# Who makes the first chunk's block sums, and in which order w2's operands come, in a Hymba-style layer on one core

## The chip, the cores and the metric

The kernel runs on one core of a Trainium2 chip. The metric is the device time of one launch in microseconds (us); smaller is better. The engines are named as the profile names them: PE (TensorE's matmuls), PEld (its weight loads), DVE (VectorE), ACT (ScalarE), POOL (GpSimd) and SP (the queue that issues most DMAs).

## The reference, cut to what matters

One layer of a decoder trunk for 1024 tokens of width 1024 in float32. It has two SwiGLU feed-forward networks (width 2816) around a mixer of attention and a gated recurrence:

```python
x = x + 0.5 * _swiglu(_rms_norm(x, ffn1_norm), ffn1_w1, ffn1_w3, ffn1_w2)
...                                   # mixer: attention and HGRN2, one output projection
x = x + 0.5 * _swiglu(_rms_norm(x, ffn2_norm), ffn2_w1, ffn2_w3, ffn2_w2)

def _swiglu(h, w1, w3, w2):
    return (jax.nn.silu(h @ w1) * (h @ w3)) @ w2
```

The change touches the last product of a SwiGLU, the one with w2, at its start. As there are two networks, it acts at two places of the run.

## The kernel before

**Precision and products.** Every float32 operand is split into a high part (a CAST on ACT, line 108) and a low part (a subtraction, line 109, on DVE or POOL), and each product of two operands is three matmuls: high by high, high by low, low by high. A block product is a Strassen-like scheme with seven products in place of eight, numbered 0 to 6. The operands of a product are sums and differences of blocks.

**hidden()** makes silu(h w1) * (h w3) in eleven steps `fp`, each with two halves `wi`; its outputs are turned into the seven operands `g` of the next product by tail() (POOL sums on lines 312 to 317, splits on ACT and DVE) and stored to DRAM tensors `gd`.

**back()** is the product with w2, for both networks. The inner dimension is cut into four chunks (`CHUNKS = (3, 3, 3, 2)`), the tokens into four groups q. A round r is one chunk; group(r, q, cs) multiplies the products `cs` of one token group: for each product c the stored operand `gp` comes back by DMA (fetch, line 600, eight products ahead) and is the stationary side, and w2's operand `o{c}` is the moving side; each such product is nine matmuls of 128x512 (line 637; six in the last chunk). Banks: products 0 and 1 accumulate in bank `ya`, 4, 5, 6 in `yb`, 3 and 2 in `yc`. After product 0, ACT copies bank `ya` to a total (line 617) *before* product 1 may accumulate in it; the other banks are copied or added to `acc` on ACT (622) and DVE (624).

**w2's operands.** load() brings four blocks of a chunk, here called by their places (0,0), (0,1), (1,0), (1,1). step(ch, c) splits the source block of product c into `o{c}`. Three of the sources are sums made in place. prep() makes the first ones per piece k: (0,1) = (1,1) - (0,1) on line 553, then (0,0) = (0,1) + (0,0) on line 554; they are what products 5 and 4 read. others() makes the later ones: (1,0) = (1,0) - (0,0) on line 563 and (0,0) = (1,1) - (0,0) on line 564, for products 6 and 3. So others() must come after product 4's and product 1's splits have read the blocks.

**Order.** Inside `manual_schedule` each engine runs its instructions in the order in which they are recorded. At the start of back() the code loads chunk 0 of w2, fetches the first eight `gp`, records the splits of products 0, 2 and 1 and prep(0), and mixes in what is left of hidden(): `before[0]`, `before[1]` (the last two evacuations, lines 362 and 365 on DVE and 278 on POOL) and `before[2]` (the last tail()), whose pieces go into a list `todo`. work() takes pieces from `todo`, done() all that a product needs. The tail's first piece is the split into a tile named `spare`, whose source is the POOL sum of line 312.

**Which products come first.** TURN sets from which group on a product belongs to a round: in round 0 the groups hold products 0 and 2; 0, 4, 1 and 2; 0, 4, 1, 5, 3 and 2; and all seven.

Of the kernel before, what the change touches and what calls it, by code (L numbers as in the profile page):

```python
# [56 lines left out]
CHUNKS = (3, 3, 3, 2)  # L57
# [28 lines left out]
def hymba_kernel(ctx: ExitStack, tc: tile.TileContext, a, out, stop=None):  # L86
    nc = tc.nc
# [434 lines left out]
    def back(i, load, spots, sg, wa, wb, wc, go, so, ac, ps, before, fetch_x, add_x, moments, finish, final):  # L522
# [12 lines left out]
        def sooner(n):  # L535
            for _ in range(n):
                if early:
                    early.pop(0)()
# [4 lines left out]
            while any(w[0] == (ch, c) for w in todo):  # L543
                work(1)

        def prep(ch):

            b11, b12, b22 = b[ch][0, 0], b[ch][0, 1], b[ch][1, 1]

            def first(k):  # L550
                def go():
                    done(ch, 0)
                    nc.gpsimd.tensor_sub(b12[k], b22[k], b12[k])  # L553
                    nc.gpsimd.tensor_add(b11[k], b12[k], b11[k])
                return go

            early.extend(first(k) for k in range(CHUNKS[ch]))
# [9 lines left out]
        def step(ch, c, eng=None):  # L567

            b11, b12, b21, b22 = (b[ch].get(e) for e in ((0, 0), (0, 1), (1, 0), (1, 1)))
            src = {0: b11, 4: b11, 1: b21, 5: b12, 3: b11, 6: b21, 2: b22}[c]  # L570
            o = ops[ch, c] = so.tile([P, 3, 2, 512], F32R, tag=f"o{c}", name=f"o{c}_{ch}")

            def piece(k):
                def go():
                    if c == 4:
                        sooner(len(early))
                    split(o[:, k, 0, :], o[:, k, 1, :], src[k], eng)
                    if c == 1 and ch:
                        others(ch, k)()
                return go  # L580

            todo.extend(((ch, c), piece(k)) for k in range(CHUNKS[ch]))
# [2 lines left out]
        seq = []  # L585
        for r in range(nch + 1):
            for q in range(4):
                cs = [(c, r if q >= TURN[c] else r - 1) for c in ORDER]
                seq.append((r, q, [(c, ch) for c, ch in cs if 0 <= ch < nch]))
        flat_seq = [(q, c, ch) for r, q, cs in seq for c, ch in cs]  # L590
        parts = {}
# [81 lines left out]
                add_x(acc[m // 2][:, m % 2 * 512:m % 2 * 512 + 512], xt.pop(m))  # L673

        with tc.manual_schedule(engines=ORDEREDY):
            b[0] = load(0, ((0, 0), (1, 1), (0, 1), (1, 0)))
            for k in range(AHEAD):
                fetch(k)
            step(0, 0, nc.gpsimd)
            step(0, 2)  # L680
            step(0, 1)
            work(len(todo))
            prep(0)
            sooner(len(early))
            before[0]()
            before[1]()
            rest = before[2]()
            step(0, 4)

            spare = so.tile([P, 3, 2, 512], F32R, tag="o6", name="spare")  # L690
            spots.extend([lambda k=k: [flat(spare[:, k])] for k in range(2)] +
                         [lambda t=t: [acc[t].bitcast(F32R)] for t in (2 * TOKENS[3], 2 * TOKENS[3] + 1)] +
                         3 * [lambda: [wb.tile([P, 512], F32R, tag="c", name=f"go_{m}", bufs=NC) for m in range(2)]])
            todo.extend((None, f) for f in rest[:3])
            todo.extend(((0, 3), others(0, k)) for k in range(CHUNKS[0]))
            todo.extend((None, f) for f in rest[3:])
            for c in (5, 3, 6):
                step(0, c)
            for r, q, cs in seq:
                group(r, q, cs)  # L700
                moments.get((r - nch, q), lambda: None)()
                if (r, q) == (nch - 1, 3) or r == nch and q < 3:
                    todo.extend((None, f) for f in finish(2 * TOKENS[q] + 1, 2 * TOKENS[q], acc))
            final(work)
# [792 lines left out]
```

## Time and profile before

| what | value |
|---|---|
| median of 3 runs | 2055.58 us (2055.48 to 2057.73) |
| the profiled execution's own time | 2058.68 us |
| its span, first to last instruction | 2056.8 us |
| PE busy | 1966.5 us, 96% of the span, 9344 matmuls |
| DVE busy | 1328.2 us, 65% |
| ACT busy | 751.0 us, 37% |
| POOL busy | 827.2 us, 40% |
| mean granted TensorE clock | 0.984 of full speed |

The times of the trace are us from the first instruction. The first network's product with w2 begins at 483.7 us, the second one's at 1822.4 us. A share of busy time is an average over stages; what the change can move is read at those two places.

### The profile page before, as it was taken

How to read it: one execution, taken by the hardware profiler on the slowest of the kernel's cores; microseconds unless marked ns; L12 is line 12 of the kernel's file. 1: busy time of each engine (PE TensorE's matmuls, PEld its weight loads, DVE VectorE, ACT ScalarE, POOL GpSimd, SP SyncE). 2: the span in 40 equal slices, each digit the busy share in tenths (PEclk: the TensorE clock that was granted, in tenths of full speed). 3: DMA queues.
4: the chain of work that ended last, by engine and by line, in shares of the span. 5: the costliest groups of instructions: out<-in, count | busy, mean ns of one | idle time of the engine just before them, and what ended most of it. 6: DMA issues, size and time to landing. Idle time of an engine off the chain costs nothing. (4 is left out here: it accounts for less than half of the span.)

```text
span 2056.8 us, 25751 instructions
## 1 busy us (share of the span) xinstructions
PE 1966.5 (96%) x9344; PEld 1620.4 (79%) x9344; DVE 1328.2 (65%) x2044; ACT 751.0 (37%) x1373; POOL 827.2 (40%) x698
## 2 busy tenths in 40 slices
PE   6889999998999989999999998989899999989998
PEld 5678888886788778888899997777688888867886
DVE  8566766678566665565666767364667666775664
ACT  6333334334311243323434435143343343353112
POOL 6555655556333340000222222053555555664452
PEclk9999999999999999999999999999999999999999
DMA  3144444447887521111001002321444444478875
GB/s 143 41 154 154 143 144 155 153 149 266 295 289 236 198 98 39 35 39 47 16 17 31 9 1 94 132 83 41 145 159 148 144 145 158 143 268 301 290 233 191
DMA packets 160878, 284.07 MB, mean 138 GB/s; under 512 B 10865, under 2 KB 90225, under 8 KB 160753
## 3 DMA queue, kind: packets, MB, share of 16 engines
q1 hardware_dynamic: 158160, 273.53, 39.8%
q10 hardware_dynamic: 2592, 8.91, 1.1%
q8 instruction: 74, 1.21, 0.2%
q14 instruction: 52, 0.42, 0.1%
HBM read 189.08 MB, written 93.32 MB: 137 GB/s over the span
## 5 line engine op out<-in xcount | busy, mean ns | idle before, releaser
L255 PE MATMUL bb<-cb,wparts 128*128 128x512 f32 x1584 | 398.8, 401 | 24.3 <-DVE u L350 12.9
L255 PEld LDWEIGHTS bb<-cb,wparts 128*128 128x128 f32 x1584 | 301.5, 191 | 101.6 <-ACT wparts L108 13.6
L255 PE MATMUL ba<-cb,wparts 128*128 128x512 f32 x1056 | 263.5, 400 | 5.3 <-DVE cb L170 2.6
L255 PE MATMUL bc<-cb,wparts 128*128 128x512 f32 x1056 | 261.6, 396 | 0.0
L255 PEld LDWEIGHTS ba<-cb,wparts 128*128 128x128 f32 x1056 | 200.9, 191 | 54.9 <-DVE cb L170 2.9
L255 PEld LDWEIGHTS bc<-cb,wparts 128*128 128x128 f32 x1056 | 199.0, 189 | 48.9 <-DVE wparts L109 0.4
L109 DVE TENSOR_TENSOR wparts<-s,wparts 128x512 fp32r<-128x512 f32 x176 | 153.4, 874 | 98.6 <-ACT wparts L108 98.6
L637 PE MATMUL yb<-o,gp 128*128 128x512 f32 x792 | 203.9, 400 | 8.9 <-DVE o L109 7.9
L637 PEld LDWEIGHTS yb<-o,gp 128*128 128x128 f32 x792 | 149.2, 189 | 48.2 <-DVE o L109 11.2
L972 PE MATMUL pj<-hH,hw 128*128 128x512 f32 x480 | 171.0, 413 | 4.8 <-ACT hw L108 3.6
L108 ACT CAST o<-b 128x512 fp32r<-128x512 f32 x148 | 83.6, 621 | 246.6 <-PE yb L637 172.1
L109 DVE TENSOR_TENSOR go<-g,go 128x512 fp32r<-128x512 f32 (+1 forms) x152 | 155.5, 1028 | 14.5 <-ACT go L108 14.4
L109 DVE TENSOR_TENSOR wparts<-raw,wparts 128x512 fp32r<-128x512 f32 x116 | 117.3, 1012 | 43.9 <-ACT wparts L108 42.7
L109 DVE TENSOR_TENSOR o<-b,o 128x512 fp32r<-128x512 f32 x144 | 129.4, 911 | 17.4 <-ACT o L108 17.3
L637 PE MATMUL yc<-o,gp 128*128 128x512 f32 x528 | 135.5, 398 | 3.6 <-DVE acc L624 1.6
L1147 PE MATMUL apj<-aw,hH 128*128 128x384 f32 x512 | 138.8, 352 | 0.0
L637 PE MATMUL ya<-o,gp 128*128 128x512 f32 x528 | 135.7, 400 | 2.9 <-ACT ya L617 2.9
L108 ACT CAST wparts<-s 128x512 fp32r<-128x512 f32 x176 | 106.0, 618 | 78.6 <-POOL s L338 37.8
L338 POOL TENSOR_TENSOR s<-raw 128x512 f32<-128x512 f32 x44 | 70.7, 1608 | 147.3 <-DVE wparts L109 87.8
L637 PEld LDWEIGHTS yc<-o,gp 128*128 128x128 f32 x528 | 99.6, 189 | 29.9 <-ACT o L108 2.5
L637 PEld LDWEIGHTS ya<-o,gp 128*128 128x128 f32 x528 | 100.2, 190 | 28.2 <-ACT ya L617 3.3
L972 PEld LDWEIGHTS pj<-hH,hw 128*128 128x128 f32 x480 | 91.7, 191 | 24.9 <-ACT hw L108 3.8
(256 smaller groups left out, 3358.2 us busy)
## 6 DMA issues: line engine op xcount, KB each, us to landing
gd<-go SPq DMA_DIRECT2D x140, 512.0 KB, 3.2
gp<-gd SPq DMA_DIRECT2D x168, 384.0 KB, 4.8
raw<-in_ffn_w SPq DMA_DIRECT2D x88, 512.0 KB, 3.7
b<-in_ffn_w SPq DMA_DIRECT2D x22, 768.0 KB, 7.0
gp<-gd SPq DMA_DIRECT2D x56, 256.0 KB, 3.0
hraw<-in_w_hg SPq DMA_DIRECT2D x32, 256.0 KB, 2.6
araw<-in_w_at SPq DMA_DIRECT2D x16, 384.0 KB, 3.1
b<-in_ffn_w SPq DMA_DIRECT2D x10, 512.0 KB, 5.3
```

The source lines that it names most:

```text
L108: nc.scalar.copy(rhi, src)
L109: (eng or nc.vector).tensor_sub(rlo, src, rhi.bitcast(F32))
L255: mm(bank, w[:, wj, ks], cb[c][:, :, bj, ks], start=(start and k == 0 and (wj, bj) == (0, 0)), stop=(k == 3 and wj == 1), skip_group_check ...
L338: nc.gpsimd.tensor_tensor(out=s[j], in0=s[0] if x is None else x, in1=s[1] if y is None else y, op=getattr(ALU, op))
L637: mm(bank[x], v[:, k, wj, :], o[:, k, bj, :], start=(new and k == 0 and (wj, bj) == (0, 0)), stop=(k == n - 1 and wj == 1), skip_group_che ...
L972: mm(u[hf], w[k // 4][:, wj, k % 4, :], r[hf][:, k, :], start=(k == 0 and (wj, r) == (0, hH)), stop=(k == KT - 1 and wj == 1))
L1147: mm(pj, l[t // 4][:, k, tsl], w[:, j, :], start=(n == 0), stop=(n == 3 * KT - 1))
```

## The change

In the first chunk of w2, in both networks: prep(0) records its six sums (lines 553, 554) on DVE where they were on POOL; others(0, k) are recorded at once where they were spread in `todo` after three pieces of the tail; the block (0,1) is loaded second and (1,1) third; product 4's split comes before product 1's; products 5, 3 and 6 are split in the order 5, 3, 6 as before, but with one piece of the tail after 5 and the other pieces after 3; and in the first two groups of round 0 the products run in the order 0, 2, 4, 1 (before: 0, 4, 1, 2). All other chunks stay as they were.

```diff
-        def prep(ch):
+        def prep(ch, eng=nc.gpsimd):
...
-                    nc.gpsimd.tensor_sub(b12[k], b22[k], b12[k])
-                    nc.gpsimd.tensor_add(b11[k], b12[k], b11[k])
+                    eng.tensor_sub(b12[k], b22[k], b12[k])
+                    eng.tensor_add(b11[k], b12[k], b11[k])
...
-                cs = [(c, r if q >= TURN[c] else r - 1) for c in ORDER]
+
+                cs = [(c, r if q >= TURN[c] else r - 1) for c in (ORDER if r or q > 1 else (0, 2, 4, 1))]
...
-            b[0] = load(0, ((0, 0), (1, 1), (0, 1), (1, 0)))
+            b[0] = load(0, ((0, 0), (0, 1), (1, 1), (1, 0)))
             for k in range(AHEAD):
                 fetch(k)
             step(0, 0, nc.gpsimd)
             step(0, 2)
+            work(len(todo))
+            prep(0, nc.vector)
+            sooner(len(early))
+            step(0, 4)
             step(0, 1)
             work(len(todo))
-            prep(0)
-            sooner(len(early))
+            for k in range(CHUNKS[0]):
+                others(0, k)()
             before[0]()
             before[1]()
             rest = before[2]()
-            step(0, 4)
...
-            todo.extend((None, f) for f in rest[:3])
-            todo.extend(((0, 3), others(0, k)) for k in range(CHUNKS[0]))
-            todo.extend((None, f) for f in rest[3:])
-            for c in (5, 3, 6):
-                step(0, c)
+            step(0, 5)
+            todo.append((None, rest[0]))
+            step(0, 3)
+            todo.extend((None, f) for f in rest[1:])
+            step(0, 6)
```

What this does to three engines' orders at the start of back() in the first network (the second is alike). `b00`, `b01`, `b10`, `b11` are the tiles that hold the blocks, `g10_..` the last step's gates, `o4_0` product 4's operand of chunk 0.

POOL before, from the last piece of product 0's low part on:

```order
L109 TENSOR_TENSOR o0_0_3774<-b00_0__3749,o0_0_3774 128x512
L553 TENSOR_TENSOR b01_0_3754<-b11_0_3752,b01_0_3754 128x512
L554 TENSOR_TENSOR b00_0_3748<-b01_0_3754,b00_0_3748 128x512
...
L278 TENSOR_TENSOR g10_1_3555<-g10_1_3555,c110_1_3620 128x512
L278 TENSOR_TENSOR g10_0_3509<-g10_0_3509,u210_1_3642 128x512
L312 TENSOR_TENSOR g10_0_3509<-g10_0_3509,g10_1_3555 128x512
...
L563 TENSOR_TENSOR b10_0_3756<-b10_0_3756,b00_0_3748 128x512
```

and with the change:

```order
L109 TENSOR_TENSOR o0_0_3774<-b00_0__3749,o0_0_3774 128x512
L563 TENSOR_TENSOR b10_0_3756<-b10_0_3756,b00_0_3748 128x512
L564 TENSOR_TENSOR b00_0_3748<-b11_0_3754,b00_0_3748 128x512
...
L278 TENSOR_TENSOR g10_1_3555<-g10_1_3555,c110_1_3620 128x512
L278 TENSOR_TENSOR g10_0_3509<-g10_0_3509,u210_1_3642 128x512
L312 TENSOR_TENSOR g10_0_3509<-g10_0_3509,g10_1_3555 128x512
```

Six instructions stood ahead of the gates' last products (278) and the sum of line 312, and six stand there now; but these are the later sums, which wait for product 4's and product 1's splits, and the first sums are gone to DVE.

DVE with the change, from product 2's low part on (before, product 1's low part came next, then lines 362 and 365, then product 4's):

```order
L109 TENSOR_TENSOR o2_0_3775<-b11_0_3754,o2_0_3775 128x512 x3
L553 TENSOR_TENSOR b01_0_3752<-b11_0_3754,b01_0_3752 128x512
L554 TENSOR_TENSOR b00_0_3748<-b01_0_3752,b00_0_3748 128x512
...
L109 TENSOR_TENSOR o4_0_3794<-b00_0_3748,o4_0_3794 128x512 x2
L109 TENSOR_TENSOR o4_0_3794<-b00_0__3749,o4_0_3794 128x512
L109 TENSOR_TENSOR o1_0_3795<-b10_0_3756,o1_0_3795 128x512 x3
L362 TENSOR_TENSOR c110_1_3620<-bb10_1_3625,c110_1_3620 128x512
L365 TENSOR_TENSOR u210_1_3642<-bc10_1_3680,u210_1_3642 128x512
L109 TENSOR_TENSOR o5_0_3822<-b01_0_3752,o5_0_3822 128x512 x3
```

The six sums now stand between product 2's and product 4's low parts, and product 5's low part comes ahead of the tail's.

ACT with the change, from the copy of the first `ya` bank on:

```order
L618 COPY ya0_3837<-ya0_0_3827 128x512
...
L108 CAST spare_3821<-g10_0_3509 128x4x128
L618 COPY ya1_3873<-ya0_1_3863 128x512
L108 CAST o3_0_3823<-b00_0_3748 128x512 x2
...
L623 COPY acc0_7_3738<-yb0_1_3900 128x512 x2
...
L618 COPY ya2_3958<-ya0_2_3948 128x512
```

The cast into `spare` stands directly ahead of the second `ya` copy, as it did before; ahead of the third `ya` copy stand now also product 3's casts, the second piece of the tail and the two copies of `acc0_7`, which wait for a DVE addition.

On SP the load of (0,1) moves up past five stores of `gd` (from behind them to ahead of them), the other two loads keep their places, the `gp` of product 2 for the second group moves ahead of those of 4 and 1, and two later `gp` move ahead of stores from `spare`.

## Rows read from the trace of the kernel before

**Rows 1.** Windows: both w2 starts, and 1 us of TensorE's slow stretch; PEclk is granted clock.
```profile
483.70:520.90 37.20, 30.04 (x110) 21.80 (x109) 30.84 (x29) 17.36 (x35) 23.96 (x16) 0.91 0.82 278
1822.40:1858.20 35.80, 28.61 (x110) 20.95 (x109) 27.13 (x28) 17.41 (x36) 24.91 (x17) 0.95 0.83 282
...
63.00:64.00 1.00, 1.00 (x4) 0.81 (x3) 0.83 (x2) 0.47 (x1) 0.00 (x0) 0.50 0.00 0
```

**Rows 2.** Timeline of PE, first network: start, length, what, [idle before <-releaser].
```profile
483.71 2.26 PE L637 MATMUL ya<-o,gp 128*128 128x512 f32 x9
...
492.51 0.95 PE L637 MATMUL yb<-o,gp 128*128 128x512 f32 x3 [2.10 <-DVE o L109]
...
496.90 2.66 PE L637 MATMUL ya<-o,gp 128*128 128x512 f32 x9
...
510.78 3.27 PE L637 MATMUL yb<-o,gp 128*128 128x512 f32 x8 [2.59 <-DVE o L109]
...
518.67 2.37 PE L637 MATMUL yc<-o,gp 128*128 128x512 f32 x9 [0.78 <-DVE acc L624]
520.88 2.26 PE L637 MATMUL ya<-o,gp 128*128 128x512 f32 x9
```

**Rows 3.** Timeline of PE, second network.
```profile
1822.37 2.26 PE L637 MATMUL ya<-o,gp 128*128 128x512 f32 x9
...
1835.24 3.75 PE L637 MATMUL ya<-o,gp 128*128 128x512 f32 x9 [2.87 <-ACT ya L617]
...
1858.16 2.26 PE L637 MATMUL ya<-o,gp 128*128 128x512 f32 x9
```

**Rows 4.** Timeline of DVE, first network.
```profile
479.04 0.69 DVE L278 TENSOR_TENSOR g<-g,u 128x512 f32<-128x512 f32 x1
479.65 10.31 DVE L109 TENSOR_TENSOR o<-b,o 128x512 fp32r<-128x512 f32 x6
489.89 0.68 DVE L362 TENSOR_TENSOR c<-bb,c 128x512 f32<-128x512 f32 x1
490.49 0.68 DVE L365 TENSOR_TENSOR u<-bc,u 128x512 f32<-128x512 f32 x1
...
510.05 2.49 DVE L109 TENSOR_TENSOR o<-b,o 128x512 fp32r<-128x512 f32 x4
```

**Rows 5.** Timeline of POOL, first network.
```profile
479.27 1.61 POOL L553 TENSOR_TENSOR b<-b,b 128x512 f32<-128x512 f32 x1 [1.05 <-DMA b<-in_ffn_w]
...
487.79 1.63 POOL L554 TENSOR_TENSOR b__3749<-b,b__3749 128x512 f32<-128x512 f32 x1
...
493.67 1.60 POOL L312 TENSOR_TENSOR g<-g,g 128x512 f32<-128x512 f32 x1
...
531.59 1.30 POOL L553 TENSOR_TENSOR b<-b,b 128x512 f32<-128x512 f32 x1 [22.08 <-DMA gp<-gd]
...
534.22 1.29 POOL L553 TENSOR_TENSOR b<-b,b 128x512 f32<-128x512 f32 x1
```

**Rows 6.** Timeline of ACT, first network.
```profile
477.13 1.67 ACT L108 CAST o<-b 128x512 fp32r<-128x512 f32 x3 [2.24 <-DMA b<-in_ffn_w]
...
486.01 0.59 ACT L617 COPY ya<-ya 128x512 f32<-128x512 f32 x1 [3.15 <-PE ya L637]
486.49 0.59 ACT L622 COPY acc<-ya 128x512 f32<-128x512 f32 x1
...
495.31 0.62 ACT L108 CAST spare<-g 128x512 fp32r<-128x512 f32 x1 [5.24 <-POOL g L312]
495.83 0.58 ACT L617 COPY ya<-ya 128x512 f32<-128x512 f32 x1
...
501.64 1.35 ACT L108 CAST go<-g 128x256 fp32r<-128x256 f32 x4
```

**Rows 7.** Timeline of PE after its longest idle stretch, early in the run.
```profile
61.95 5.49 PE L255 MATMUL bb<-cb,wparts 128*128 128x512 f32 x12 [8.64 <-ACT wparts L108]
...
70.25 2.96 PE L255 MATMUL bb<-cb,wparts 128*128 128x512 f32 x12
```

## The prediction

> **What bounds the kernel now.** TensorE sets the end of this run; it stands still in few places, and two of them are the starts of the product with w2. I read first the windows over these two stretches: PE is busy 30.04 of 37.20 us in the first network and 28.61 of 35.80 in the second [rows 1]. Then the timeline of PE, which says what a gap costs in all. Nine matmuls of one product are due every 2.10 us (each row of nine is 2.26 long with the tail of its last matmul, and the next row starts 2.10 later where nothing waits). Twelve products lie between the first w2 matmul and the first one of the fourth token group, so that one should come 12 x 2.10 = 25.2 us after the first. It comes at 520.88 - 483.71 = 37.17 us in the first network [rows 2] and at 1858.16 - 1822.37 = 35.79 us in the second [rows 3]. So 12.0 and 10.6 us are lost, **22.6 us in all, the most that any change here can win**. From there on PE is the engine that the others wait for, so I take it that what is won or lost up to this point moves the end one for one.
>
> The reader should see three waits in it. Product 4's operand is late: PE idles 2.10 us for DVE's low parts [rows 2], because POOL's six first sums run from 479.27 to 489.42 [rows 5]. Then the second `ya` product of the group starts at 496.90 and 1835.24; in the second network the view names its releaser, ACT's copy of line 617 [rows 3]. That copy stands in ACT's queue right behind the cast into `spare`, and this cast waited until 495.31 for the POOL sum of line 312 [rows 6], which ended at 493.67 + 1.60 = 495.27 [rows 5]. So a piece of the old network's tail, for which nobody is in a hurry, holds a copy for which PE waits. Third, product 5's and 3's operands are late: 2.59 us idle and eight matmuls at 3.27 us [rows 2].
>
> **Prices.** DVE's subtraction of two SBUF tiles takes 2.49 / 4 = 0.62 us while POOL idles and 10.31 / 6 = 1.72 us while it works [rows 4]. POOL's takes (534.22 - 531.59) / 2 = 1.31 us while DVE idles, and (487.79 - 479.27) / 5 = 1.70 us beside DVE [rows 5]. DVE's readings of PSUM stay at 490.49 - 489.89 = 0.60 us beside POOL [rows 4]. An ACT copy takes 486.49 - 486.01 = 0.48 us, a cast 495.83 - 495.31 = 0.52 [rows 6].
>
> **The change part by part**, with the first network's times; z is the first w2 matmul, 483.71.
>
> (1) First sums on DVE. DVE is free for product 2's low parts at 479.65, as now [rows 4]; its casts began at 477.13 [rows 6]. POOL has ended product 0's low parts 1.05 us before 479.27 [rows 5] and now has nothing to do, so DVE runs at its fast price: three low parts, 1.9, to 481.5; six sums, three of them waiting for the one before (I take the full length of 0.69 for these [rows 4]), 3.9, to 485.5; product 4's three low parts to 487.3. Product 4 is first wanted at z + 4 x 2.10 = 492.1, since product 2 now goes ahead of it. **The wait for product 4 is gone**, with 4.8 us to spare. The first low part of product 1 is done at 487.95.
>
> (2) Later sums on POOL. They overwrite what product 1's low parts read, so POOL starts at 488.0 and not before. Beside it DVE has two low parts of product 1, the two PSUM readings of lines 362 and 365, and three low parts of product 5: 2 x 1.72 + 2 x 0.60 + 3 x 1.72 = 9.8, to 497.75. In the 8.6 us of SBUF work POOL does 8.6 / 1.70 = 5.0 sums and in the 1.2 us beside PSUM work 0.9, so its sixth ends at about 497.8. Behind it, alone: two products of line 278 and the sum of line 312, 3 x 1.31 = 3.95, to 501.75. Before, this sum ended at 495.27: **the tail's first sum is 6.5 us later**.
>
> (3) What waits behind it. In ACT's queue the cast into `spare` still stands ahead of the second `ya` copy, and PE needs that copy for product 1. From the sum's end to PE it took 0.04 + 0.52 + 0.58 [rows 5, 6], and with 0.06 for the semaphore 1.2, so PE goes on at 502.95, z + 19.2. It ran dry at z + 5 x 2.10 = 494.2: an idle stretch of 8.7 us. The nearest row is the early one of 8.64: after it 24 matmuls took 70.25 - 61.95 = 8.30 us where 24 x 0.233 = 5.60 was due [rows 7], 2.7 us more, at a granted clock of 0.50 [rows 1], TensorE's lower level of 1.2 GHz. So the third group starts at z + 19.2 + 2.1 + 2.7 = z + 24.0, and its second product ends at z + 28.2.
>
> (4) The third `ya` copy. Ahead of it ACT has copies that wait for DVE's addition to `acc0_6`, and that stands behind one low part of the tail, three of product 3 and another of the tail. From 502.4 on: two and a half of these beside POOL's last three sums, the rest alone, and the addition, 1.72 + 1.72 + 1.2 + 2 x 0.62 + 0.6, to 508.9. Then ACT's three copies, two casts, four short casts at 1.35 in all [rows 6] and the copy itself at 0.58, 4.4, to 513.3 = z + 29.6. PE waits 1.4 us for it. After the gap of 2.10 us three matmuls took 0.95 [rows 2], about full pace, so I count no clock here.
>
> (5) To the fourth group: three products, 6.3; the wait of the next one for DVE's addition, 0.78 before [rows 2], taken as 0.8 to 0.9; and one product, 2.1: **z + 38.8**. Products 5 and 3 no longer wait: their low parts are done at 497.75 and about 507.7.
>
> (6) The rest costs nothing. The load of (0,1) goes ahead of five stores, and POOL, which waited for it at 479.27 [rows 5], no longer does; SP's other moves follow the order in which PE now reads the operands. Twelve more operations on DVE, fewer on POOL, are inside (1). The late tail feeds stores that only the last chunk reads back.
>
> **The sum.** z + 38.8 against 37.17 and 35.79: 1.6 and 3.0 us later, 4.6 in all. The second network comes out the same after the change, since POOL's idle time removes what made the two differ. The sum is a difference inside the profiled execution (2058.68 us, span 2056.8); that lies 3.1 above the median of the runs shown, and I add it to the median: 2055.58 + 4.6 = **2060.2 us**. Of 22.6 us lost the change takes away about 10, at products 4, 5 and 3, and puts some 14 back at the `ya` copies. A difference within 0.2% (4.1 us) is about what a measurement of this kernel cannot tell from none, and the forecast is just beyond it.
>
> **Bounds.** The step that decides is POOL's pace from 488.0 to the sum of line 312. If all nine operations took 1.31, PE would go on 1.9 us sooner, and with 0.8 from (4) a start would be 2.7 shorter. If all nine took 1.70, it would be 1.2 longer. The nearest rows are the mixed ones, so I take 1.70 beside DVE. The clock after 8.7 us idle lies between 1.2 us (the eight matmuls of 510.78, 3.27 for 2.03) and 2.7; but up to 1.4 of that only shortens the wait in (4).
>
> The Trainium skill (SBUF — State Buffer, section Who interferes with whom) says that a DVE instruction with two SBUF inputs and a GpSimd one that reads SBUF take turns, the second one blocked until the first has finished. By that a pair would take 0.62 + 1.31 = 1.93 us, and the eight pairs of (2) to (4) 0.2 us more each, 1.6 per start and 2063.4 in all. The trace agrees that both slow down, but with 1.72 and 1.70 us for a pair; the rows decide.
>
> **Rivals.**
> - *The tail's sum is not late* (chance 0.07). If ACT's second `ya` copy were free of the `spare` cast, or the sum came ahead of the later sums, only the wait of 0.9 would be left at each start: 11.1 + 9.7 = 20.8 won, 2034.8 us. For it speaks only that (1) works; against it that the order shows the cast ahead of the copy and six sums ahead of line 312, and that ACT has already waited 5.24 us in this very place [rows 6]. It decides at z + 10.5: were the copy done by then, all would be won; each us later costs one.
> - *POOL is fast* (0.16). With nine operations at 1.31 a start ends at z + 36.1, 1.1 sooner than before in the first network and 0.3 later in the second: 2054.8, no change. The point from which it decides is the sum's end at 499.3. Against it: DVE has five SBUF operations in just that stretch.
> - *The second gap drops the clock too* (0.12). If the wait of (4) is 2.6 us or more, eight matmuls cost 1.24 more, as at 510.78 [rows 2]; twice, 2062.7.
> - *Full blocking* (0.05), 2063.4, as above.
>
> **How the numbers follow.** The forecast has 0.60; its own spread is about 2.5 us to either side, so 0.33 of it lies beyond 2059.7. With the two slower rivals, slower by over 0.2% has 0.50. The rest of the forecast, 0.27, and most of the fast POOL, 0.13, are within 0.2%: 0.40. Faster: 0.07 and 0.03, 0.10. The range leaves out the first rival and the ends of the others: 2055.2 to 2064.0.
>
> **What would show it.** Right: in both w2 starts one gap of 8 to 9 us ahead of the second group's product 1, released by ACT's `ya` copy, and a second of 1 to 2 us ahead of the third group's; no wait for product 4; DVE's six sums at 0.6 to 0.7 us; POOL's line 563 beginning 4 us after z and line 312 ending 18 us after it; the fourth group at z + 38 to 40. Wrong: the fourth group well below z + 36, or a `ya` copy that does not wait for POOL; or a wait for `gp`.

## The result and the profile after

The changed kernel takes **2068.55 us** (median of 4 runs, 2067.70 to 2069.75); beside it the kernel before took 2055.53 us (4 runs, 2054.20 to 2057.73). The ratio is 1.006, with a 95% interval of 1.0048 to 1.0072: slower by 0.6%, some 13 us. The forecast was 2060.2 us, with a range up to 2064.0. So the sign was right and the size was not. The profiled execution took 2069.75 us, its span is 2068.0 us, 11.2 more than the span of the kernel before.

The head of the page: the span, and busy time of each engine with its share and instructions.

```profile
span 2068.0 us, 25755 instructions
...
PE 1968.7 (95%) x9344; PEld 1625.7 (79%) x9344; DVE 1317.6 (64%) x2056; ACT 750.8 (36%) x1373; POOL 806.9 (39%) x686
```

The timeline of PE over the first start of w2 (start and length in us, what, and in brackets the idle time before it and its releaser), the counterpart of [rows 2]; z, the first w2 matmul, is 482.83 here:

```profile
482.83 2.26 PE L638 MATMUL ya<-o,gp 128*128 128x512 f32 x9
...
491.23 2.26 PE L638 MATMUL yb<-o,gp 128*128 128x512 f32 x9
502.16 5.85 PE L638 MATMUL ya<-o,gp 128*128 128x512 f32 x18 [8.67 <-ACT ya L618]
507.85 2.26 PE L638 MATMUL yb<-o,gp 128*128 128x512 f32 x9
512.44 3.73 PE L638 MATMUL ya<-o,gp 128*128 128x512 f32 x9 [2.33 <-ACT ya L618]
516.01 2.26 PE L638 MATMUL yb<-o,gp 128*128 128x512 f32 x9
...
521.22 2.37 PE L638 MATMUL yc<-o,gp 128*128 128x512 f32 x9 [0.85 <-DVE acc L625]
523.42 2.26 PE L638 MATMUL ya<-o,gp 128*128 128x512 f32 x9
```

Product 4 (`yb`, 491.23) no longer waits. Two gaps are left, both released by ACT's `ya` copy: 8.67 us ahead of the second group's product 1 and 2.33 us ahead of the third group's. Behind each of them TensorE is slow: 18 matmuls take 507.85 - 502.16 = 5.69 us where 4.20 are due, and nine take 516.01 - 512.44 = 3.57 where 2.10 are due. The fourth group comes at z + 40.59, 3.4 us later than in [rows 2].

The second network, counterpart of [rows 3], does the same, and the fourth group comes at 1868.08 - 1827.33 = z + 40.75, 5.0 us later than before:

```profile
1827.33 2.26 PE L638 MATMUL ya<-o,gp 128*128 128x512 f32 x9
...
1846.66 6.01 PE L638 MATMUL ya<-o,gp 128*128 128x512 f32 x18 [8.67 <-ACT ya L618]
...
1856.93 3.89 PE L638 MATMUL ya<-o,gp 128*128 128x512 f32 x9 [2.16 <-ACT ya L618]
...
1868.08 2.26 PE L638 MATMUL ya<-o,gp 128*128 128x512 f32 x9
```

The granted clock over the stretches behind the two gaps of the first network (columns: stretch, us, busy us of PE, PEld, DVE, ACT and POOL with instructions, PEclk, DMA share, GB/s):

```profile
502.16:507.85 5.69, 5.69 (x18) 4.54 (x19) 5.69 (x6) 2.51 (x5) 3.46 (x3) 0.73 0.52 164
...
512.44:516.01 3.57, 3.57 (x10) 2.85 (x10) 2.07 (x5) 2.08 (x5) 0.00 (x0) 0.58 1.02 298
```

Where the first gap comes from, in the timelines of DVE, POOL and ACT, the counterparts of [rows 4 to 6]. DVE's last first sum, product 5's low parts, and later the addition to `acc`:

```profile
484.14 0.69 DVE L554 TENSOR_TENSOR b__3749<-b,b__3749 128x512 f32<-128x512 f32 x1
...
490.67 4.06 DVE L109 TENSOR_TENSOR o<-b,o 128x512 fp32r<-128x512 f32 x3
...
507.38 0.68 DVE L625 TENSOR_TENSOR acc<-yb,acc 128x512 f32<-128x512 f32 x1
```

POOL's first and last later sum, and the sum of line 312 behind them:

```profile
487.37 1.63 POOL L563 TENSOR_TENSOR b<-b,b 128x512 f32<-128x512 f32 x1 [10.06 <-DVE o L109]
...
495.93 1.26 POOL L564 TENSOR_TENSOR b__3749<-b,b__3749 128x512 f32<-128x512 f32 x1
...
499.71 1.26 POOL L312 TENSOR_TENSOR g<-g,g 128x512 f32<-128x512 f32 x1
```

ACT's casts and copies between the two gaps:

```profile
501.00 0.62 ACT L108 CAST spare<-g 128x512 fp32r<-128x512 f32 x1 [10.94 <-POOL g L312]
501.53 0.58 ACT L618 COPY ya<-ya 128x512 f32<-128x512 f32 x1
...
508.09 1.07 ACT L623 COPY acc<-yb 128x512 f32<-128x512 f32 x2 [3.42 <-DVE acc L625]
...
510.56 1.34 ACT L108 CAST go<-g 128x256 fp32r<-128x256 f32 x4
511.79 0.60 ACT L618 COPY ya<-ya 128x512 f32<-128x512 f32 x1
```

POOL ends line 312 at 499.71 + 1.26 = 500.97, z + 18.1. The cast into `spare` has waited 10.94 us for it, and the second `ya` copy comes straight behind. The third one stands behind two copies of bank `yb` which wait 3.42 us for DVE's addition, and behind the tail's casts.

### The profile page after: what moved, and what is told of

Its sections match the earlier page's. It is cut to its first block, busy times and chain, and to the rows that moved or that the text cites. A ratio compares the mean times of both kernels' runs of the same rounds, so it can differ in the third digit from the quotient of the medians.

```text
span 2068.0 us, 25755 instructions
## 1 busy us (share of the span) xinstructions
PE 1968.7 (95%) x9344; PEld 1625.7 (79%) x9344; DVE 1317.6 (64%) x2056; ACT 750.8 (36%) x1373; POOL 806.9 (39%) x686
## 5 line engine op out<-in xcount | busy, mean ns | idle before, releaser
L109 DVE TENSOR_TENSOR go<-g,go 128x512 fp32r<-128x512 f32 (+1 forms) x152 | 145.9, 964 | 15.9 <-ACT go L108 15.6
L108 ACT CAST go<-g 128x512 fp32r<-128x512 f32 (+1 forms) x152 | 90.8, 604 | 56.3 <-DMA gd<-go 43.0
```

The lines of the kernel that those rows point to most:

```text
L108: nc.scalar.copy(rhi, src)
L109: (eng or nc.vector).tensor_sub(rlo, src, rhi.bitcast(F32))
```

## The experiments

All edits are made to the changed kernel unless said otherwise. Theory A, formed on these rows: a start of w2 is as long as ACT's queue makes it, by the place of two `ya` copies in it, and the clock behind the gaps adds to that. The rivals are named with the runs.

**1. The changed kernel again.** No edit.

> The changed kernel once more, unaltered, to measure how much slower it is and whether the part of the difference that lies outside the two starts of the product with w2 comes back. Theory A (all of the loss lies in the starts: +3.4 us in the first network and +5.0 in the second, 8.4 in all, by the two gaps ahead of ya products and by the clock after each of them): the median lies 8 to 9 us above that of the kernel before, and the rest of the 13.0 us seen so far was chance in where TensorE's clock drops elsewhere. Rival C (some 3 to 5 us are lost outside the starts, whatever the reason): 12 to 14 us above it again.

Median 2069.09 us against 2057.23; the ratio is 1.0064 (1.0051 to 1.0078), 11.9 us. The starts were 40.60 and 40.91 us long. Theory A's 8 to 9 us are too few: some 3 us lie elsewhere, and the result is near rival C's 12 to 14.

**2. The cast into `spare` moved behind product 3's pieces.**

```diff
-            todo.append((None, rest[0]))
             step(0, 3)
-            todo.extend((None, f) for f in rest[1:])
+            todo.extend((None, f) for f in rest)
```

> One piece is moved: the tail's first put (the cast into spare that waits for line 312) is recorded behind product 3's three operand pieces instead of ahead of them. Theory A (the wait is a matter of ACT's queue: a ya copy stands behind a cast that waits for POOL): product 1 of the second group now starts at z + 10.5 with no gap, since its ya copy no longer stands behind the cast; but all of the tail's pieces then stand ahead of the third group's ya copy, POOL's sums end no sooner (line 317 at z + 22.9 in the changed kernel), and the one gap comes back there: product 1 of the third group at z + 26 to 29, the fourth group at z + 39 to 41, total 2065 to 2070 us. Rival B (the time is set by POOL and DVE holding each other up over the later sums, wherever the copies stand): the gap ahead of product 1 of the second group stays at 8 to 9 us, and the total at 2068.5.

Median 2065.52 us, ratio 1.0047 (1.0032 to 1.0061). PE's timeline, with z = 483.50:

```profile
494.01 4.36 PE L638 MATMUL ya<-o,gp 128*128 128x512 f32 x18
498.21 2.26 PE L638 MATMUL yb<-o,gp 128*128 128x512 f32 x9
511.55 4.21 PE L638 MATMUL ya<-o,gp 128*128 128x512 f32 x9 [11.08 <-ACT ya L618]
```

Product 1 of the second group starts at z + 10.51 without a gap, and the 18 matmuls take 4.36 us at full pace. The whole wait has moved to the third group, 11.08 us, and the fourth group comes at z + 39.95. Theory A holds and rival B falls: POOL ended line 312 even later (z + 19.5 against z + 18.1 in the changed kernel), and yet the gap is gone, since the copy no longer stands behind the cast in ACT's queue. Taking a wait away here moved it by one group.

**3. POOL's order turned round.**

```diff
-            for k in range(CHUNKS[0]):
-                others(0, k)()
             before[0]()
             before[1]()
             rest = before[2]()
+            for k in range(CHUNKS[0]):
+                others(0, k)()
```

> POOL's order alone is turned round: the tail's two products of line 278 and its sum of line 312 are recorded ahead of the six later sums. Theory A: POOL waits for DVE's line 365 (z + 7.9 in the changed kernel) and ends line 312 about 3 x 1.27 us later, z + 11.8, so the cast into spare and the second ya copy follow at once and product 1 of the second group starts at z + 13, with a gap of 2 to 3 us instead of 8.7. The six later sums then end some 4 us later than now, product 3's casts wait for them in ACT's queue ahead of the third ya copy, and the gap moves to the third group: its product 1 at z + 28 to 31, the fourth group at z + 40 to 43, total 2067 to 2074. Rival B: what counts is that POOL's later sums are late; with them later still, both gaps stay and the total is 4 us per start higher, about 2076. Rival D (only the first gap matters): the total falls by about 7 us per start, to 2055.

Median 2070.33 us, ratio 1.0069 (1.0055 to 1.0082). z = 483.92:

```profile
496.08 4.47 PE L638 MATMUL ya<-o,gp 128*128 128x512 f32 x18 [1.50 <-ACT ya L618]
500.39 2.26 PE L638 MATMUL yb<-o,gp 128*128 128x512 f32 x9
514.08 3.83 PE L638 MATMUL ya<-o,gp 128*128 128x512 f32 x9 [11.43 <-ACT ya L618]
```

The first gap falls to 1.50 us, and a gap of 11.43 us stands at the third group, z + 30.16. The fourth group comes at z + 41.25, in the second network at z + 42.57. Whichever of the two is first on POOL, the other one's late casts stand ahead of a `ya` copy. Rival B (both gaps stay, 2076 us) and rival D (2055 us) fall.

**4. Four short casts of the tail one product later.**

```diff
-                work(2 if r in (0, nch) else 1)
+                work({(1, 3): 0, (2, 0): 4}.get((q, j), 2) if r == 0 else 2 if r == nch else 1)
```

> Two pieces of the tail (four short casts of 256 columns into go tiles) are recorded one product later, so that they no longer stand ahead of the third ya copy in ACT's queue; they took 1.23 us there. Theory A with the clock (the second gap, 2.33 and 2.16 us in the changed kernel, costs its own length and then 1.5 us more because the granted clock drops after it): the second gap shrinks to 0.9 to 1.1 us and the nine matmuls behind it run at full pace, 2.10 us instead of 3.57 and 3.73, so each start is 2.7 us shorter and the total 2063 us. If the clock drops after a gap of 1 us too, only the 1.2 us per start come back: 2066. Rival (the copy waits for something else than its place in the queue): no change, 2068.5.

Median 2065.63 us, ratio 1.0047 (1.0034 to 1.0060). PE behind the second gap in both networks, z = 483.40 and 1823.96:

```profile
511.81 2.36 PE L638 MATMUL ya<-o,gp 128*128 128x512 f32 x9 [1.06 <-ACT ya L618]
514.14 2.36 PE L638 MATMUL yb<-o,gp 128*128 128x512 f32 x9
...
1852.35 2.38 PE L638 MATMUL ya<-o,gp 128*128 128x512 f32 x9 [0.65 <-ACT ya L618]
```

The gaps are 1.06 and 0.65 us and the clock stays up: nine matmuls take 2.33 us. The starts are 38.24 and 38.23 us, 2.4 and 2.7 less than in run 1, as theory A has it. But the total gained 3.5 us and not 5: from the fourth group to the end of the product PE now needs 193.93 and 192.16 us (run 1: 192.25 and 190.88). The ratio's interval overlaps that of run 1, so it is the traces that show the gain. New waits stand in the second chunk; these are the first network's:

```profile
550.40 2.37 PE L638 MATMUL yc<-o,gp 128*128 128x512 f32 x9 [1.30 <-DVE acc L625]
...
557.63 2.34 PE L638 MATMUL ya<-o,gp 128*128 128x512 f32 x9 [0.66 <-issue]
```

**5 and 6. One network alone.** The whole change under `if i == 0:`, then under `if i == 1:`.

> The change is made in the first network alone; the second one's start with w2 is as in the kernel before. Theory A (each start loses by itself, by the gaps in ACT's queue and the clock after them): first start z + 40.6 to the fourth group, second start z + 35.8 as before, total 3.4 us over the kernel before, some 2060. Rival C (a good part of the loss lies outside the starts and comes with the change as a whole): total 2062 to 2066, with the two starts at the same lengths.

> The change is made in the second network alone; the first one's start is as in the kernel before. If what the change costs adds up (5.0 us were measured for the first network alone, about 12 for both), this one costs 6 to 7: 2063 to 2064. By the starts alone (z + 40.7 against z + 35.8 to the fourth group): 5.0 us, 2062. The first start should come at 37.2 us as before.

First network alone: 2062.17 us against 2057.13, ratio 1.0024 (1.0015 to 1.0034), 5.0 us. Second alone: 2061.94 against 2056.84, ratio 1.0027 (1.0018 to 1.0036), 5.1 us. Both starts are slower by themselves. The forecasts were 3.4 us for the first alone and 5.0 or 6 to 7 for the second. Unexpected: in both profiled executions the second gap was as long as before or longer, and the clock stayed up. The first network's rows (z = 484.28), and the granted clock behind that gap:

```profile
503.63 5.78 PE L638 MATMUL ya<-o,gp 128*128 128x512 f32 x18 [8.69 <-ACT ya L618]
...
513.92 2.36 PE L638 MATMUL ya<-o,gp 128*128 128x512 f32 x9 [2.41 <-ACT ya L618]
516.12 2.26 PE L638 MATMUL yb<-o,gp 128*128 128x512 f32 x9
```

```profile
513.92:516.12 2.20, 2.20 (x10) 1.80 (x11) 1.37 (x4) 2.09 (x5) 0.00 (x0) 1.00 0.99 223
```

Nine matmuls take 2.20 us after 2.41 us idle at a clock of 1.00; in the changed kernel's profile they took 3.57 after 2.33 at 0.58. So the fourth group came at z + 39.26 and, in the other run, z + 39.44, 1.3 and 1.5 us sooner than in run 1. Run 5 lost all of that again and run 6 part of it: PE now waits for an addition to `acc` ahead of the last product of the fifth group. That product in run 5 and, below it, in the changed kernel:

```profile
552.45 2.36 PE L638 MATMUL yc<-o,gp 128*128 128x512 f32 x9 [1.44 <-DVE acc L625]
```

```profile
550.95 2.37 PE L638 MATMUL yc<-o,gp 128*128 128x512 f32 x9
```

It comes at z + 68.17 in run 5 and at z + 68.12 in the changed kernel (68.1 to 68.9 in its four profiled executions). In run 6 it comes at z + 67.96 after a wait of 1.05 us, against z + 68.4 to 68.8 in the second network of the four.

**7. The first sums back on POOL**, all else as changed.

```diff
-            prep(0, nc.vector)
+            prep(0)
```

> The first sums alone go back to POOL; the order of the pieces, of the loads and of the products stays as changed. Theory A: POOL makes the six first sums again, so product 4's and product 1's low parts come later on DVE, POOL's later sums start 2 to 4 us later, line 312 ends 2 to 4 us later, and as ACT's queue still has the cast into spare ahead of the second ya copy, product 1 of the second group starts at z + 21.5 to 23 and the fourth group at z + 43 to 44.5: 2073 to 2076 us in all. So DVE's share of the change is a gain of 2 to 4 us per start, and the loss comes from the rest. Rival E (DVE's six sums are themselves what costs, by holding up DVE's other work): each start gets shorter, towards z + 36 to 37, total 2058 to 2061.

Median 2072.41 us, ratio 1.0070 (1.0056 to 1.0084). Product 1 came at z + 21.11 and z + 21.92 instead of 19.33, the fourth group at z + 41.01 and z + 41.83. Rival E, by which each start gets shorter, falls: DVE's sums bring product 1 some 2 us sooner and are not what costs. At the fourth group they win less than expected, because without them the second gap is only 0.99 and 1.55 us and the clock stays up behind it. The median is the highest of all, but the ratio's interval overlaps that of run 1, so it is not shown that the total lost by it.

**8. The order of the products as before**, all else as changed.

```diff
-... for c in (ORDER if r or q > 1 else (0, 2, 4, 1))]
+... for c in ORDER]
```

> Only the special order of the second group's products is undone (0, 4, 1, 2 again instead of 0, 2, 4, 1); all else stays as changed. Theory A: with product 2 ahead of product 4, acc0_6 is written first from yc, so the part from yb is added by DVE, behind three low parts and two of the tail, and ACT's two copies of the same bank wait for this addition, the third ya copy behind them: that is the second gap. With product 4 ahead of 2 those copies need no DVE addition. So PE still stands still ahead of product 1, from z + 8.4 to z + 19.3 (10.8 us), but there is no second gap, or one below 0.5 us: the fourth group at z + 38 to 39 and 2064 to 2065 us in all. Rival F (the second gap comes from the tail's casts alone): a gap of 1 to 2 us stays ahead of the third group's product 1 and the fourth group comes at z + 40 to 41, total 2068.

Median 2067.14 us, ratio 1.0050 (1.0035 to 1.0066). PE's waits over the first start (engine and line, what it waited for: us in total, times, longest us) hold one `ya` copy instead of two:

```profile
PE ya L638 <- ACT ya L618: 10.7, 1, 10.7
PE yc L638 <- DVE acc L625: 0.9, 1, 0.9
```

There is no second gap, and the fourth group comes at z + 39.12 and z + 38.94. So it is product 2 ahead of product 4 that puts ACT's copies of `yb` behind a DVE addition, and the third `ya` copy behind them; rival F falls. The total is 2 us below run 1, where 4 to 5 were expected, and the two ratios' intervals overlap.

**9. The tail behind the third copy.** With the products' order as before:

```diff
-                work(2 if r in (0, nch) else 1)
+                work((0, 0, 0, 1, 4, 4)[j] if (r, q) == (0, 2) else 2 if r in (0, nch) else 1)
...
-            for e, at in (((0, 0), (2, 0)), ((1, 1), (2, 2)), ((1, 0), (2, 5)), ((0, 1), (3, 1))):
+            for e, at in (... if r else (((0, 0), (2, 5)), ((1, 1), (3, 0)), ((1, 0), (3, 1)), ((0, 1), (3, 2)))):
...
-            todo.append((None, rest[0]))
-            step(0, 3)
-            todo.extend((None, f) for f in rest[1:])
-            step(0, 6)
             for r, q, cs in seq:
                 group(r, q, cs)
+                if (r, q) == (0, 0):
+                    step(0, 3)
+                if (r, q) == (0, 1):
+                    todo.extend((None, f) for f in rest)
+                if (r, q) == (0, 2):
+                    step(0, 6)
```

> What theory A asks for in full: DVE's first sums and POOL's order as changed; the products' order as before; product 3's pieces recorded behind the first group; all pieces of the tail recorded behind the third ya copy, most of them after the third group's product 3; product 6's pieces behind the third group; and the loads of the second chunk's blocks three to four products later, since they overwrite tiles that the tail reads. Theory A: neither of the two gaps is left, the wait for DVE's addition to acc of 0.9 us stays, the fourth group at z + 26 to 27 (12 products and 0.9 us are 26.1), 14 us per start less than in the changed kernel; some of it is given back where the tail's low parts and stores and the later loads meet the fourth group and the second chunk, 2 to 4 us per start. Total 2042 to 2048 us. Rival B (POOL and DVE beside each other are the limit): the third group waits for product 5's or 3's low parts instead, the fourth group at z + 34 or later, total 2056 or more.

Median 2055.83 us, ratio 0.9992 (0.9983 to 1.0001): no difference from the kernel before. The starts are 27.05 and 26.38 us, 14 less than in the changed kernel, as expected. But 8.3 and 7.0 us more than in run 1 are spent behind the fourth group (200.54 and 197.89 us), not 2 to 4. In the first network (z = 482.76):

```profile
522.40 3.91 PE L638 MATMUL yb<-o,gp 128*128 128x512 f32 x9 [1.93 <-ACT acc L623]
...
541.41 2.36 PE L638 MATMUL yb<-o,gp 128*128 128x512 f32 x9 [2.51 <-ACT acc L623]
```

ACT's copies stand there behind casts of the second chunk's operands, which wait for that chunk's loads.

**10 and 11. The second chunk's loads ahead of the tail's last stores, and its first sums on DVE.** Run 10, from run 9:

```diff
-            for e, at in (... if r else (((0, 0), (2, 5)), ((1, 1), (3, 0)), ((1, 0), (3, 1)), ((0, 1), (3, 2)))):
+            for e, at in (... if r else (((0, 0), (2, 5)), ((1, 1), (2, 5)), ((0, 1), (2, 5)), ((1, 0), (3, 0)))):
...
-                for p, (_, store) in zip(pieces[1:], r):
+                for p, (_, store) in zip(pieces[1:5], r):
                     p.append(store)
+                pieces[7:] = [[store] for _, store in r[4:]]
...
-                    todo.extend((None, f) for f in rest)
+                    todo.extend((None, f) for f in rest[:7])
                 if (r, q) == (0, 2):
                     step(0, 6)
+                    todo.extend((None, f) for f in rest[7:])
```

and run 11 also has

```diff
-                    prep(r + 1)
+                    prep(r + 1, nc.gpsimd if r else nc.vector)
```

> As the run with the tail behind the third copy, with two things more: the second chunk's loads are recorded within the third group again and one behind the other, and the last three stores of the tail are recorded behind product 6's pieces, so that they do not stand ahead of these loads in SP's queue. Theory G (what the shorter starts won, 13.5 us each, was given back in the second chunk, because SP's queue brought its blocks late: the loads left at z + 30 to z + 40 behind ten stores, POOL's sums of the second chunk started at z + 52, and PE waited three to five times): the starts stay at 27 us, the loads leave at z + 28 to z + 34, the fifth group no longer waits for an ACT copy, and the total falls to 2036 to 2044 us. Rival H (the loads are limited by the transfers' rate, not by their place in the queue, or by the tiles that they overwrite): the waits stay, 2052 to 2056 us.

> The same, and VectorE makes the first sums of the second chunk too. Theory G: where these sums are still the last thing that product 4 of the second chunk waits for, six sums of 0.65 us in place of 1.3 to 1.6 us bring its operand 4 us sooner: 1 to 2 us per start less than without this, 2034 to 2042. Rival: DVE has its own work there (additions to acc, low parts), and the sums ahead of them in its queue hold these up: the same or up to 2 us more.

Run 10: **2041.40 us against 2056.84, ratio 0.9931 (0.9918 to 0.9945)**, 15 us below the kernel before. Run 11: 2042.45, ratio 0.9932 (0.9920 to 0.9945), the same within its interval, so it is not POOL's sums that the second chunk waits for. The four loads in the view of their line (times, durations in ns, first and last start in us), in the changed kernel and in run 10:

```profile
L505 SPq DMA_DIRECT2D b<-in_ffn_w x4: 383/446/626, 515.8 to 528.5; - x4
```

```profile
L506 SPq DMA_DIRECT2D b<-in_ffn_w x4: 494/598/1088, 511.0 to 514.0; - x4
```

In the changed kernel they left between z + 33.0 and z + 45.7, in run 9 between z + 30.1 and z + 40.4, in run 10 (z = 481.62) between z + 29.4 and z + 32.4. From the fourth group on run 10 needs 193.47 and 191.72 us, 7.1 and 6.2 less than run 9, so theory G holds and rival H falls. PE's waits that are left there up to the second chunk:

```profile
505.80 2.36 PE L639 MATMUL yc<-o,gp 128*128 128x512 f32 x9 [0.91 <-DVE acc L626]
...
527.31 2.36 PE L639 MATMUL ya<-o,gp 128*128 128x512 f32 x9 [0.25 <-DVE ya L621]
...
532.98 2.36 PE L639 MATMUL yc<-o,gp 128*128 128x512 f32 x9 [1.22 <-DMA gp<-gd]
```

**12 to 16. More executions of both kernels.** No edits; the first is the kernel before, with times as well (2056.18 us, ratio 0.9997, 0.9988 to 1.0006).

> The kernel before, unaltered, profiled once more, for the lengths of its own stretches in a second execution. If the 2.8 us by which the two profiled executions differed outside the starts are chance: this execution differs from the first one by up to 2 us in the same stretches (the hidden products, the stretch between the networks, the end), with both starts at 37 and 36 us again. If they come with the change: its stretches outside the starts agree with the first execution within 0.5 us, and the second chunk shows no wait of PE for an addition to acc.

> One more profiled execution of the changed kernel. Theory J (the clock after a gap of 2.3 us is a matter of chance: it fell in four of six such gaps seen so far in the changed start, and where it stayed the fourth group came at z + 39.3 to 39.4): the fourth group at z + 40.6 to 40.9 or at z + 39.2 to 39.5 in each network, nothing between. The stretch between the two w2 products, 1111.6 and 1112.1 us in two executions of this kernel and 1109.9 and 1106.2 in two of the kernel before: if the change shifts it, it is 1111 to 1112.5 here too; if it is chance, anything from 1106 to 1112.

> The same as the look before it: z + 40.6 to 40.9 or z + 39.2 to 39.5; 1111 to 1112.5 us between the two w2 products if the change shifts that stretch, 1106 to 1112 if it is chance.

> One more profiled execution of the kernel before. Theory J: the fourth group at z + 35.5 to 37.3. The stretch between the two w2 products: 1106 to 1110 us if the change shifts it, 1106 to 1112 if it is chance.

> The same as the look before it: z + 35.5 to 37.3; 1106 to 1110 us between the two w2 products if the change shifts that stretch, 1106 to 1112 if it is chance.

With the first profiles and run 1 there are four executions of each kernel. Us from the trace, by stretch; "rest" is from the fourth group to the last w2 matmul, "between" from there to the next w2 product:

| execution | span | to z | start 1 | rest 1 | between | start 2 | rest 2 | end |
|---|---|---|---|---|---|---|---|---|
| before | 2056.8 | 483.7 | 37.2 | 191.6 | 1109.9 | 35.8 | 190.4 | 8.2 |
| before, c4 | 2050.4 | 481.4 | 36.0 | 192.2 | 1106.2 | 35.5 | 190.8 | 8.2 |
| before, d3 | 2056.4 | 483.5 | 37.3 | 191.5 | 1109.4 | 35.8 | 190.9 | 8.2 |
| before, d4 | 2054.8 | 482.3 | 36.1 | 192.1 | 1109.8 | 35.6 | 190.8 | 8.2 |
| after | 2068.0 | 482.8 | 40.6 | 191.8 | 1112.1 | 40.8 | 190.8 | 9.1 |
| after, a1 | 2067.4 | 482.2 | 40.6 | 192.3 | 1111.6 | 40.9 | 190.9 | 9.0 |
| after, d1 | 2067.1 | 483.8 | 41.3 | 191.8 | 1109.7 | 40.0 | 191.4 | 9.0 |
| after, d2 | 2069.9 | 484.0 | 41.2 | 192.8 | 1111.3 | 40.7 | 190.9 | 9.0 |

By the means of four the span is 13.5 us longer: 4.3 in the first start and 4.9 in the second, together 9.2; 2.4 between the two products; and 0.5, 0.3, 0.3 and 0.9 before z, in the two rests and at the end. Theory J's "nothing between" missed: three of the four starts of d1 and d2 came at z + 40.0, 41.2 and 41.3, as their first gaps were 9.21 to 9.45 us. Between the two products d1's 1109.7 us lies outside the 1111 to 1112.5 that a shift by the change was to give.

## Why the prediction was wrong

The path through the queues was right; two steps failed. Step (4) counted no clock behind the second gap, and a slow clock there cost about 1.5 us per start, so the fourth group came late. Step (6) put the rest at nothing; where the clock stayed up as forecast, waits in the second chunk took that time back, all of it in run 5 and part of it in run 6. Some 4 us lie in neither, and their cause stays open.

**(1) DVE's first sums: right.** Six sums were done at z + 2.0 (forecast 1.8), and product 4 does not wait. Run 7, without it, has product 1 at z + 21.1 and z + 21.9 instead of z + 19.3.

**(2) POOL: right.** It began at z + 4.5 (4.3), and line 312 ended at z + 18.1 (18.0). The price of 1.70 us beside DVE was met by 1.60 to 1.83 in the timeline of POOL. DVE's price was not met: product 5's three low parts took 4.06 / 3 = 1.35 us each where 1.72 was taken, and DVE was done at z + 11.9, not z + 14.0. That POOL's end still came right is in part luck, since five sums at its slow price had been worked out from DVE's 8.6 us of work. The 0.60 us for DVE's reading of PSUM was taken from a stretch in which POOL stood idle, from 489.42 [rows 5] to its first product of line 278 at 490.65; beside a busy POOL it was 490.67 - 490.08 = 0.59 here, so the figure holds. The rival of a fast POOL is out. Full blocking does not show in these rows: POOL's five sums took (495.93 - 487.37) / 5 = 1.71 us each. The rule of the Trainium skill (SBUF — State Buffer, section Who interferes with whom) gives an estimate of 0.62 + 1.31 = 1.93 us for a pair that takes whole turns.

**(3) The first gap: right, its clock not.** Product 1 came at z + 19.33 (19.2) after 8.67 us (8.7), behind the cast into `spare`; run 2 shows that this place in the queue made the gap. The clock behind it cost 5.69 - 4.20 = 1.5 us, not 2.7. In the 12 starts of this pattern, with first gaps of 8.66 to 9.45 us, the 18 matmuls took 5.78 to 7.11 us against the 4.36 of run 2, so 1.4 to 2.8: the row I took [rows 7] is the upper end of what came.

**(4) The third copy: right, its clock not. This step failed for the starts.** PE went on at z + 29.61 and z + 29.60, as forecast with z + 29.6 (so near by luck too: the other six starts of the changed kernel had z + 29.6 to 30.4). The prediction had "so I count no clock here"; the nine matmuls behind it took 3.57 and 3.73 us instead of 2.10. Steps (3) and (4) hang together: ACT sets the time at which PE goes on, so what the first drop costs only shortens the second gap. As it cost 1.2 us less, PE stood still 2.33 us and not 1.4. The drop that delays the fourth group is the one behind the last gap, and that one I had set to zero. The rival that has it there was in the text, with a chance of 0.12 and a threshold of 2.6 us. Runs 4, 5, 6 and 8 tell the rest: with gaps of 1.06 and 0.65 us the start is 38.2 us, with 2.41 and 2.40 us and no drop 39.3 and 39.4, with no second gap 39.1 and 38.9. The forecast of z + 38.8 is about the changed kernel without that drop.

**(5) The sum.** The starts are z + 40.9 and z + 40.6 in the mean, 2.1 and 1.8 above z + 38.8. And the first start before was z + 36.6 in the mean of four, where the one profile that I had showed 37.17; with 0.1 in the second network this adds 0.7. Together 4.6 of the missing 8 us.

**(6) "The rest costs nothing": wrong. This step failed too.** The tail's pieces do not only feed stores that are read back late. The load of the second chunk's first block waits for DVE's low parts of the tail (1.0 us in run 4), and the tail's stores stand ahead of the other loads in SP's queue. So that chunk comes late: POOL begins its sums at z + 55.9 to 57.7 in the changed kernel's four executions, at z + 47.9 to 49.4 in the kernel before. By the means of four, each rest is only 0.3 us longer in the changed kernel. But where PE gets through the third group sooner, it waits in the second chunk: the rests of run 4, with waits for additions to `acc`, are 1.3 to 1.7 us longer than those of run 1, and in run 9, with waits for ACT's copies too, 7 to 8 us. So a clock that stayed up would have won little. In run 5 it did, the start was within 0.5 us of the forecast, and from z to the last w2 matmul it took 39.26 + 194.06 = 233.3 us, against 232.4 to 234.0 in the changed kernel's four first networks. In run 6 it took 230.9 in the second network, against 231.4 to 231.8. Runs 9 and 10 show that short starts pay once the second chunk's loads come in time.

**What stays open.** The prediction took it that what is lost up to the fourth group moves the end one for one. In the profiled executions about 4 of the 13.5 us lie outside both starts and rests, 2.4 of them between the two products, in instructions that the change does not touch. At the end, 0.9 us, ACT's last outputs wait for a store of `xo` in all four executions (2.87 to 3.03 us) where they waited for a DVE addition before (2.05 to 2.06); why stays open. Between the products one place can be seen, a short stretch of the mixer, in the profile before and in the one after:

```profile
981.60:987.00 5.40, 3.50 (x24) 3.18 (x23) 2.78 (x10) 2.27 (x4) 1.23 (x2) 1.00 0.01 3
```

```profile
983.00:990.00 7.00, 5.92 (x23) 5.42 (x22) 3.11 (x11) 3.11 (x7) 1.96 (x5) 0.51 0.01 2
```

The same work runs at a clock of 1.00 in the one and at 0.51, the level of 1.2 GHz, in the other, after waits for the same DVE instruction. "Between" runs from 1106.2 to 1109.9 us in four executions before and from 1109.7 to 1112.1 in four after, so the ranges overlap. Runs 2, 3 and 4, which have the change in both networks, had 1108.4 to 1109.5; run 10, the fastest kernel, had 1111.5, and run 6, with half the change, 1107.4. So it is not shown that the change shifts this stretch; the cause of the 2.4 us stays open.

## What to carry to other kernels

When work moves to another engine, follow each queue behind it: what stands behind a piece that now waits, and who needs that? Pieces that nobody is in a hurry for (here the old network's tail) belong behind the copies that TensorE waits for, on ACT, POOL and SP alike; moving only one of them moves the wait one group on, and runs 2 and 3 won little or nothing.

Where a late copy sets the time at which TensorE goes on, a slow clock after an earlier gap only shortens the wait for that copy, and a slow clock after the last gap delays what follows; price that one, and let the range hold it both ways. What the delay costs in the end is decided by the next operands: here they came late, so that the product ended no sooner in run 5 and only 0.5 to 0.9 us sooner in run 6. Follow the delayed stores and loads to the next chunk before the rest is put at nothing.

One profiled execution is no base for half a per cent: the code between the two products, which no edit touches, took 1106 to 1112 us in these runs, and 1106.2 to 1109.9 in four executions of one kernel.

## What the runs showed of the hardware

The clock behind a gap is not set by the gap's length alone. Of nine second gaps of 1.86 to 2.41 us at this place, the clock fell behind seven (nine matmuls in 3.5 to 3.7 us, where full speed takes 2.1 to 2.2) and stayed at full speed behind the two longest, 2.40 and 2.41 us. Behind five of 0.65 to 1.55 us at this place it stayed. Elsewhere it stayed behind a first gap of 1.83 us (run 3, second network, 2.19 us for nine), and fell behind one of 1.54 us that followed two of 0.73 (the kernel before, second network, in c4 and d4: 3.51 and 3.29 us for nine, with a granted clock of 0.65 over the first 2 us in c4). The Trainium skill (TensorE: Matmul & The Clock Gate, Part 1: The HAM clock gate) says that the watch on TensorE's activity is free-running and does not start anew with the kernel, so that the point of a transition differs from run to run. The traces agree in that the clock fell behind some and not behind others of like gaps, a difference of about 1.4 us per gap; they do not show why.
